# One layer of a streaming encoder: tokens turned by halves, sums of weights moved one block forward, state updates on quarters of rows

## The chip, the core and the metric

The kernel runs on one core of one Trainium2 chip, in one launch. The metric is device time in microseconds (us), the median of several executions. One further execution is recorded by the hardware profiler, and all lines of a profile come from that one.

The engines have short names in the profile: PE is the matrix engine (TensorE), PEld its loads of stationary operands, DVE the vector engine, ACT the scalar engine, POOL GpSimd, and SP the engine that here issues most of the DMA transfers.

## What is computed

The reference is one layer of a hybrid encoder. It gets a prompt of 2048 tokens and a batch of 8 samples with 16 tokens each, all 1024 wide:

```
for (x, states) in (prompt, empty), (samples, carried):
    q, k, v, o, i, f, qa, ka, va = split(x @ w_in)
    hm = sigmoid(o) * head_norm(mlstm(q, k, v, i, f, C0, n0, m0))   # 4 heads x 128
    ha = window_attention(rope(qa), rope(ka), va, caches, sinks)    # 8 q heads, 2 kv heads x 64
    h  = layer_norm(alpha * x + concat(hm, ha) @ w_out)
    u  = h @ w_up                                                   # 1024 -> 2 * 2816
    c  = b_conv + causal_conv3(u)
    a, g = split(c)
    y  = layer_norm(alpha * h + (silu(g) * a) @ w_down)
```

The outputs are y for prompt and samples, and the new states: the memory C, n, m of the mLSTM, the last keys and values, and the last two rows of u. For each sample and head, the state of C with n beside it is updated as `decay * C + sum over tokens of weight * k v`; this is the part that the change calls the batch's states.

## The kernel before, in words

The 128 tokens of the samples form a tile of their own (tile 16) beside 16 prompt tiles of 128 tokens. Four stages follow one another on PE.

1. **Input projection**, four blocks of four prompt tiles each (`IBLOCKS`), the first with the sample tile as well. It is done in the manner of Strassen: each output group g (0 to 4) of a block is seven products s with sums of weight quarters and of token quarters (`i_product`, L703), and each 32-bit product is made of three products with operands split into a high and a low part. PE is at this from the start to about 628 us.
2. **Output projection**, five blocks (L222 to L224), to about 910 us.
3. **Up projection** (`f_ups`, L1853), three token blocks of 5 or 6 tiles, 22 column groups j, seven products each, to about 1849 us. It also applies the conv and the gate.
4. **Down projection** (`f_downs`, L2065), to about 2315 us.

Into the first two stages the recurrences are woven: window attention, the chunks of the mLSTM and the sample's step (`t_sample`) are generators, and a planner (`Chains`) puts their next part behind a product, by a cost and a due time that each `yield` names. The order on PE is the order of the code. On the other engines a scheduler places the instructions, by priority and by when their inputs are ready; DMA transfers are issued from SP's queue, unless ACT is named, and wait there in order.

These places matter for the change:

- **The batch's states** (`t_sample`, L1426 to L1448). For each of the 4 heads, `weighted` makes v times each sample's weight for all 128 tokens (L1426, 8 samples x 129 columns, in three pieces of 3, 3 and 2 samples). PE computes the read-out `pnum` (L1440, L1443), POOL scales the old state (L1444), PE makes three products of all 128 rows (L1447), and DVE adds these to the state (L1448). Weights are zero except for a sample's own 16 tokens, so in a product over 128 rows only 16 rows of each sample's columns count.
- **Sums of weights** (`d_sums`, L843 to L855). The down projection, also in the manner of Strassen, needs sums of quarters of w_down. For each of 11 row pairs, step 0 loads two tiles of 512 KB into buffers shared with the block's tokens (`xr1`, `xr3`), step 1 subtracts four times on DVE, step 2 stores the two results to DRAM. Before, the first eight are spread over blocks 2 and 3 of the input projection: in each of the groups 0 to 3 the three steps stand behind products 6, 5, 3 (6, 2, 5 in group 3). The last three follow in the output projection.
- **Passage to the up projection** (`run`, L263 to L276; `f_hT`, L1690; `f_tokens`, L1719). While the last output block runs, `f_hT(0)` loads six tiles of normalised tokens on ACT's queue, PE turns each of them in two halves of 512 columns (L1713), and ACT copies the result into `hraw` (L1714). `f_tokens` then forms the token operands: a step 1, 7, 6, 2, 5, 3 or 4 splits a quarter into high and low (L217 on ACT, L218 on DVE), a step t1 to t4 subtracts quarters in place (L1728 to L1734). All steps that the first products need are called at one point, i == 15. `f_next` forms the weight operands, with sums at L1772 to L1775 from the tiles `wv` and `wg`, loaded at L1752 and L1754.
- **Passage to the down projection** (end of `f_ups`). `d_weights` loads a piece of w_down and splits it, and `d_tokens` forms the token operands from the quarters `r1` to `r4` (L2017 to L2027). Both are called behind the last seven products of the up projection.
- **Loads of the down projection** (`d_begin`, `d_load`). A table says behind which call of `d_tokens` each piece of a quarter is loaded. For the first block the second quarter is loaded in one go where `f_downs` begins.

Of the kernel before, what the change touches and what calls it, by code (L numbers as in the profile page):

```python
# [8 lines left out]
F32 = mybir.dt.float32  # L9
# [5 lines left out]
P = 128  # L15
D = 1024
KD = D // P
SEQ = 2048
DB = 8
DS = 16  # L20
# [5 lines left out]
NFF = FF // P  # L26
# [178 lines left out]
class Prog:  # L205
# [20 lines left out]
    def run(self):  # L226
        PS = bass.MemoryType.PSUM
        nb = len(OBLOCKS)
        with ExitStack() as es:
            def enter(*a, **k):  # L230
                cm = self.pool(*a, **k)
                return cm.__enter__(), cm
            close = lambda cm: cm.__exit__(None, None, None)
            self.cp = es.enter_context(self.pool("const"))
            self.dp = es.enter_context(self.pool("dram", space=bass.MemoryType.DRAM))
            es.enter_context(self.tc.manual_schedule(engines={mybir.EngineType.PE}))
            self.setup()
# [12 lines left out]
            wx, wxcm = enter("wx1sb")  # L250
            self.unit_more(wx)
            self.mp, mcm = enter("osb")
            self.o_setup()
            for b in range(nb - 1):
                chains.weave(self.late_done(self.o_block(b)))
            chains.until(NPT - 1)
            chains.drain()
            close(tpcm)
            close(tcm)
            self.fp, fcm = enter("fsb", side="right")  # L260
            self.fup, fpcm = enter("fup", 3, PS)
            self.f_setup()
            dense = self.o_block(nb - 1)  # L263
            first = self.f_hT(0)
            next(first)
            n = 0
            for i, _ in enumerate(dense):
                if i >= 2:
                    next(first, None)
                if i == 15:  # L270
                    self.f_tokens(0, 1, "t1", "t3", 7, "t2", 6)

                if i >= 22 and n < (2, 4, 5)[min((i - 22) // 4, 2)]:
                    self.f_next()
                    n += 1
            for _ in first:  # L276
                pass
            assert not self.norms
            close(mcm)
            close(wxcm)  # L280
            close(xcm)

            self.wx, wxcm = enter("wx2sb")
            self.f2, f2cm = enter("f2sb")
            self.f3, f3cm = enter("f3sb")
            self.f_ups(n)
            close(f3cm)
            close(f2cm)
            self.f2, f2cm = enter("dsb")
            self.f_downs()  # L290
            for cm in (f2cm, wxcm, fpcm, fcm):
                close(cm)
# [293 lines left out]
    def i_dense(self):  # L586
# [34 lines left out]
        for item in self.items:  # L621
# [56 lines left out]
            with self.tc.issue_after(behind) if behind and b == 0 else nullcontext():  # L678
                self.advance()

            if b >= nb // 2 and g < last:

                steps = (6, 2, 5) if g == last - 1 else (6, 5, 3)
                if s in steps:
                    self.d_sums(sums, steps.index(s))
                    sums += s == steps[2]
        self.sums = sums
        self.logs_of(nb - 1)
        self.chains.hold = False
# [672 lines left out]
    def t_sample(self):  # L1362
# [52 lines left out]
            nc.gpsimd.memset(q, 0.0)  # L1415
        yield 1900, 6000
        num = []
        last = lambda w, h, b0, n: w[:, h, DS - 1::DS].rearrange("p (b o) -> p b o", o=1)[:, b0:b0 + n].to_broadcast([P, n, 129])

        def weighted(h):  # L1420

            vws = []
            for tag, b0 in zip((("qh", "ql", "qa"), ("mixa", "v1", "hn"))[h % 2], (0, 3, 6)):
                nb = min(3, DB - b0)
                vw = self.work(tag, [P, nb, 129], bufs=2 if tag == "v1" else 1, name="vws")
                V.tensor_mul(vw, v1[:, h:h + 1, :].to_broadcast([P, nb, 129]), last(dt, h, b0, nb))  # L1426
                vws.append((vw, b0, nb))
            return vws
        vws = weighted(0)
        for j in range(2):  # L1430
            ps = self.bank([P, 2, 129], "pnum")
            for i in range(2):
                h = 2 * j + i
                cn = states[h]
                if h + 2 < MH:
                    states.append(state(h + 2))
                q = qm[h % 2]
                dg = bass.AP(q.tensor, q.offset, [list(q.ap[0]), [64, DB // 2], [32 + DS, 2], [1, DS]])
                V.tensor_copy(dg, qw[:, h].rearrange("p (c b l) -> p c b l", b=2, l=DS))
                nc.tensor.matmul(ps[:, i], sd[:, h], v1[:, h], start=True, stop=False, skip_group_check=True)  # L1440
                for r in range(2):
                    for c in range(DB // 2):
                        nc.tensor.matmul(ps[32 * c:32 * c + 32, i], q[:, 2 * c + r], cn[:, 2 * c + r], start=False, stop=r == 1, skip_group_check=True)  # L1443
                nc.gpsimd.tensor_mul(cn, cn, last(wi, h, 0, DB))  # L1444
                for vw, b0, nb in vws:
                    pc = self.bank([P, 3, 129], "pcs")
                    nc.tensor.matmul(pc[:, :nb].rearrange("p b e -> p (b e)"), ktok[:, h], vw.rearrange("p b e -> p (b e)"), start=True, stop=True)  # L1447
                    V.tensor_add(cn[:, b0:b0 + nb], cn[:, b0:b0 + nb], pc[:, :nb])  # L1448
                nc.sync.dma_start(a["cn_s"][:, h], cn)
                vws = weighted(h + 1) if h + 1 < MH else None  # L1450
                yield 2800, 3500
            num.append(ps)
        hn = self.m_norm(num, emt, og)
        load = self.swa_dma(t)
# [235 lines left out]
    def f_hT(self, b):  # L1690

        nc, fp = self.nc, self.fp
        self.hraw[b] = R = fp.tile([P, KD, 768], F32, name="hraw", tag="hraw", bufs=1)
        tiles = FBLOCKS[b]
        hs = {}


        tags = ["hst", "hst"] if b else ["hh1", "hl1", "hh7", "hl7", "hh6", "hl6"]

        def load(ti):  # L1700
            if ti < len(tiles):
                tag = tags[ti] if ti < len(tags) else "hst"
                hs[ti] = fp.tile([P, D], F32, name="hst", tag=tag, bufs=2 if tag == "hst" else 1)
                (nc.sync if b else nc.scalar).dma_start(hs[ti], self.zh[tiles[ti]])

        for ti in range(len(tags)):
            load(ti)
        yield
        for ti in range(len(tiles)):
            for i in range(2):  # L1710
                ps = self.fup.tile([P, 4, P], F32, name="fht", tag="fht", bufs=2)
                for k in range(4):
                    nc.tensor.transpose(ps[:, k], hs[ti][:, (4 * i + k) * P:(4 * i + k + 1) * P], self.ident)  # L1713
                nc.scalar.copy(R[:, 4 * i:4 * i + 4, ti * P:(ti + 1) * P], ps)  # L1714
                if i == 1:
                    load(ti + len(tags))
                yield

    def f_tokens(self, b, *steps):  # L1719
# [74 lines left out]
    def f_ups(self, n):  # L1794
# [11 lines left out]
        for i, (b, j, s) in enumerate(self.seq):  # L1806
# [23 lines left out]
                self.f_tokens(b + 1, *{1: (1, "t1", "t3"), 7: (7, "t2"), 6: (6,), 2: (2,), 5: (5, "t4"), 3: (3,), 4: (4,)}[s])  # L1830
            if b == nb - 1 and j == NFF - 3 and s == 6:
                self.d_begin()
            if b == nb - 1 and j == NFF - 1 and s not in (1, 7):
                self.d_weights()
                if s != 4:
                    self.d_tokens()
        nc.sync.dma_start(self.a["conv_p"], self.prev.rearrange("p v j r -> p (v j) r"))
        nc.sync.dma_start(self.a["conv_s"], self.convs.rearrange("p v j b r -> p (v j) b r"))

# [110 lines left out]
    def d_begin(self):  # L1950
        nb = len(FBLOCKS)
        self.dseq = [(b, s, u) for b in range(nb) for s in (DLAST if b == nb - 1 else DORDER) for u in range(len(DUNITS))]
        self.dw, self.df, self.dr, self.in_down = {}, {}, {}, False
        self.nw = self.nt = self.ring = 0

        self.dq = {}
        nu = len(DUNITS)
        for u in range(nu):
            self.d_load(0, 1, u)
            for b in range(nb):  # L1960
                n = 7 * nu * b + u
                for q, at in ((1, n - 2 * nu + 4), (2, n - nu + 4), (3, n + 4), (4, n + 4)):
                    if b or q > 2:
                        self.dq.setdefault(at, []).append((b, q, u))

    def d_shape(self, b):
# [65 lines left out]
    def f_downs(self):  # L2032
# [6 lines left out]
            nc.sync.dma_start(t, a[n].to_broadcast([P, D]))  # L2039
            ln2.append(t)  # L2040
        self.in_down = True
        for u in range(len(DUNITS)):
            self.d_load(0, 2, u)
        for n in sorted(n for n in self.dq if n <= self.nt):
            for l in self.dq.pop(n):
                self.d_load(*l)
# [121 lines left out]
```

## Time and profile before

| | us |
|---|---|
| median of 3 executions | 2321.95 |
| lowest, highest | 2318.91, 2327.77 |
| profiled execution | 2324.55 |
| its span, first to last instruction | 2322.7 |
| DVE, ACT, POOL busy | 1818.9, 1274.3, 261.3 |

The span is 1.85 us shorter than the profiled execution's own time. The mean granted clock of PE is 0.996 of the full one. The DMA engines moved 272 GB/s on average.

How to read the lines: a group names the source line, engine, operation, the tile written and the tiles read. A row of a timeline begins with the start and the length in us; a bracket at its end gives the time for which its engine stood idle before it and what released it. A row of stretches has the length, then the busy time of PE, PEld, DVE, ACT and POOL with the number of instructions, then the granted clock of PE (1.00 is the full one), the mean busy share of the 16 DMA engines, and GB/s. Matmuls overlap in the pipeline, so the time from one start to the next tells more than a length does.

### The profile page before, as it was taken

The page shows a single profiled execution, that of the slowest core. Times are in us where ns is not written, and L with a number is a line of the kernel's source. Part 1 is how long each engine was busy: PE and PEld are TensorE (multiplying, and loading weights), DVE is VectorE, ACT ScalarE, POOL GpSimd, SP SyncE. Part 2 cuts the span into 40 slices and gives each one's busy share as a digit, 9 for nine tenths or more (in the row PEclk, how much of TensorE's full clock was granted, in tenths as well). Part 3 has the DMA queues.
Part 4 walks back from the last instruction along what each step waited for, and adds up shares of the span by engine and source line. Part 5 has one row for each costly group of instructions (what it writes and reads, how often), then busy time and mean ns, then how long its engine had stood idle before and what let it go on. Part 6 is the DMA issues. An engine that isn't in the chain of part 4 may idle for free. (4 is left out here: it accounts for less than half of the span.)

```text
span 2322.7 us, 39853 instructions
## 1 busy us (share of the span) xinstructions
PE 2287.1 (98%) x14293; PEld 2095.7 (90%) x14293; DVE 1818.9 (78%) x3189; ACT 1274.3 (55%) x2409; POOL 261.3 (11%) x477
## 2 busy tenths in 40 slices
PE   8999999999999999999999999999999999999998
PEld 8999989989877778999999999999999978888876
DVE  8777587787788888998778767678766786895987
ACT  5453466776766655555556545555555544444442
POOL 0001000000011111121102101013111200100200
PEclk9999999999999999999999999999999999999999
DMA  7888999999977757788777888978888776756743
GB/s 278 295 303 292 304 316 334 309 304 346 323 260 229 247 193 259 291 326 306 282 292 270 307 301 312 315 265 285 303 293 265 228 282 203 257 178 217 254 157 108
DMA packets 299877, 632.38 MB, mean 272 GB/s; under 512 B 47836, under 2 KB 141088, under 8 KB 299680
## 3 DMA queue, kind: packets, MB, share of 16 engines
q1 hardware_dynamic: 295296, 616.14, 77.3%
q0 software_dynamic: 3520, 10.56, 1.4%
q10 hardware_dynamic: 864, 3.15, 0.3%
q8 instruction: 113, 1.85, 0.3%
q14 instruction: 84, 0.69, 0.1%
HBM read 458.11 MB, written 171.64 MB: 271 GB/s over the span
## 5 line engine op out<-in xcount | busy, mean ns | idle before, releaser
L1853 PE MATMUL fup<-hh,uw 128*128 128x384 f32 (+1 forms) x1848 | 479.8, 329 | 1.7 <-ACT ua L1874 0.9
L1853 PE MATMUL dps<-hh,uw 128*128 128x384 f32 (+1 forms) x1848 | 478.2, 328 | 2.9 <-DVE u L1884 2.0
L1853 PEld LDWEIGHTS fup<-hh,uw 128*128 128x128 f32 x1848 | 330.9, 188 | 3.2 <-ACT ua L1874 1.4
L1853 PEld LDWEIGHTS dps<-hh,uw 128*128 128x128 f32 x1848 | 329.9, 188 | 3.6 <-DVE u L1884 2.2
L1910 DVE SCALAR_TENSOR_TENSOR cc<-u,cw,cc 128x768 f32<-128x768 f32 (+1 forms) x264 | 258.0, 978 | 65.6 <-ACT cc L1908 56.0
L1853 PE MATMUL fup<-hl,uw 128*128 128x384 f32 (+1 forms) x924 | 303.2, 328 | 3.1 <-DVE hl L218 3.1
L1853 PE MATMUL dps<-hl,uw 128*128 128x384 f32 (+1 forms) x924 | 302.3, 327 | 0.0
L703 PE MATMUL dps<-w,oh 128*128 128x256 f32 x1344 | 254.6, 284 | 0.9 <-DMA w<-zws 0.9
L217 ACT CAST uw<-wraw 128x1024 fp32r<-128x1024 f32 x126 | 123.0, 979 | 224.8 <-PE dps L2065 120.1
L218 DVE TENSOR_TENSOR w<-wraw,w 128x1024 fp32r<-128x1024 f32 (+2 forms) x167 | 189.2, 1139 | 53.9 <-ACT w L217 52.4
L703 PEld LDWEIGHTS dps<-w,oh 128*128 128x128 f32 x1344 | 210.6, 188 | 12.2 <-issue 8.1
L217 ACT CAST w<-wraw 128x1024 fp32r<-128x1024 f32 (+2 forms) x167 | 163.2, 984 | 105.4 <-PE dps L703 40.0
L218 DVE TENSOR_TENSOR uw<-wraw,uw 128x1024 fp32r<-128x1024 f32 x126 | 142.2, 1130 | 64.4 <-ACT uw L217 64.2
L703 PE MATMUL dps<-w,ol 128*128 128x256 f32 x672 | 187.8, 279 | 0.0
L1853 PEld LDWEIGHTS fup<-hl,uw 128*128 128x128 f32 x924 | 174.0, 188 | 3.8 <-DVE hl L218 3.7
L703 PE MATMUL dps<-oh,w 128*128 128x256 f32 x896 | 170.3, 284 | 6.3 <-ACT mr L1151 3.6
L2065 PE MATMUL fup<-uw,fu 128*128 128x512 f32 x726 | 174.0, 396 | 1.6 <-DVE uw L218 1.6
L1853 PEld LDWEIGHTS dps<-hl,uw 128*128 128x128 f32 x924 | 173.5, 188 | 0.0
L2065 PEld LDWEIGHTS fup<-uw,fu 128*128 128x128 f32 x726 | 136.3, 188 | 34.9 <-DVE uw L218 2.1
L2065 PE MATMUL dps<-uw,fu 128*128 128x512 f32 x660 | 165.3, 396 | 1.1 <-DVE uw L218 1.1
L1908 ACT ACTIVATE cc<-u,cw 128x768 f32<-128x768 f32 (+1 forms) x132 | 132.2, 1001 | 56.9 <-DVE u L1890 25.7
L703 PEld LDWEIGHTS dps<-oh,w 128*128 128x128 f32 x896 | 141.4, 190 | 13.0 <-issue 4.1
(322 smaller groups left out, 4575.6 us busy)
## 6 DMA issues: line engine op xcount, KB each, us to landing
uw<-zw SPq DMA_DIRECT2D x176, 512.0 KB, 5.2
zw<-uw SPq DMA_DIRECT2D x88, 512.0 KB, 3.4
w<-zws SPq DMA_DIRECT2D x72, 512.0 KB, 6.3
wv<-wup SPq DMA_DIRECT2D x66, 512.0 KB, 4.8
wraw<-wi SPq DMA_DIRECT2D x65, 512.0 KB, 5.0
wraw<-zt SPq DMA_DIRECT2D x60, 512.0 KB, 4.1
wraw<-wdn SPq DMA_DIRECT2D x45, 512.0 KB, 4.2
wraw<-wo SPq DMA_DIRECT2D x40, 512.0 KB, 4.7
```

Of the source, the lines that this page charges most:

```text
L217: nc.scalar.copy(hi, src)
L218: nc.vector.tensor_sub(lo, src, hi.bitcast(F32))
L703: mm(o, l, r, start=s in (1, 7) and c == k == i == 0, stop=k == 3 and i == 2, skip_group_check=True)
L1853: mm(ps, l[:, k], r[:, k], start=s in (1, 7) and k == 0 and i == 0, stop=k == 3 and i == 2, skip_group_check=True)
L1908: S.activation(c[:, v], u[:, 2:2 + n], AF.Identity, bias=w[3], scale=w[2])
L1910: V.scalar_tensor_tensor(c[:, v], u[:, i:i + n], w[i], c[:, v], op0=ALU.mult, op1=ALU.add)
L2065: mm(ps, l[:, k, c], r[:, k], start=s in (1, 4, 7) and u == 0 and k == 0 and i == 0, stop=u == nu - 1 and k == n - 1 and i == 2, skip_grou ...
```

## The change

The arithmetic result is the same; work is cut and placed in another way.

1. `t_sample`: the weighted v is made and multiplied on quarters of rows. Quarter c holds the tokens of samples 2c and 2c + 1, so each product has 32 rows and the 258 columns of those two samples. Four products, each with its own PSUM tile, take the place of three, and DVE adds two samples at a time. The cost that the chain names to the planner goes from 2800 to 2000.
2. `d_sums`: its steps stand in groups 0 to 2 of blocks 1 to 3, behind products 7, 3 and 4, until eight are made.
3. `f_hT` and `f_tokens`: the six tiles of block 0 lie in four other buffers, with eight loads instead of six. The left halves of all tiles are turned first, then the right halves of tiles 3 to 5, then of 0 to 2. The steps of `f_tokens` are called at three points (i of 4, 7 and 10).
4. `f_ups`: `d_weights` and `d_tokens` are called by the number of products left.
5. `d_begin`: the second quarter's loads are in the table, and the third and fourth come three calls later.

```diff
@@ run
-                if i == 15:
-                    self.f_tokens(0, 1, "t1", "t3", 7, "t2", 6)
+                if i in (4, 7, 10):
+                    self.f_tokens(0, *{4: (1,), 7: ("t1",), 10: ("t3", 7, "t2", 6)}[i])
@@ i_dense
-            if b >= nb // 2 and g < last:
-                steps = (6, 2, 5) if g == last - 1 else (6, 5, 3)
-                if s in steps:
-                    self.d_sums(sums, steps.index(s))
-                    sums += s == steps[2]
+            if b and g < last - 1 and sums < NK2 - 3 and s in (7, 3, 4):
+                self.d_sums(sums, (7, 3, 4).index(s))
+                sums += s == 4
@@ t_sample
         def weighted(h):
-            vws = []
-            for tag, b0 in zip((("qh", "ql", "qa"), ("mixa", "v1", "hn"))[h % 2], (0, 3, 6)):
-                nb = min(3, DB - b0)
-                vw = self.work(tag, [P, nb, 129], bufs=2 if tag == "v1" else 1, name="vws")
-                V.tensor_mul(vw, v1[:, h:h + 1, :].to_broadcast([P, nb, 129]), last(dt, h, b0, nb))
-                vws.append((vw, b0, nb))
-            return vws
+            vw = self.work(("qh", "ql")[h % 2], [P, 2, 129], name="vws")
+            for c in range(DB // 2):
+                r = slice(32 * c, 32 * c + 32)
+                V.tensor_mul(vw[r], v1[r, h:h + 1, :].to_broadcast([32, 2, 129]), last(dt[r], h, 2 * c, 2, 32))
+            return vw
...
-                for vw, b0, nb in vws:
-                    pc = self.bank([P, 3, 129], "pcs")
-                    nc.tensor.matmul(pc[:, :nb].rearrange("p b e -> p (b e)"), ktok[:, h], vw.rearrange("p b e -> p (b e)"), start=True, stop=True)
-                    V.tensor_add(cn[:, b0:b0 + nb], cn[:, b0:b0 + nb], pc[:, :nb])
+                for c0 in (0, 2):
+                    pc = [self.bank([P, 2, 129], "pcs") for _ in range(2)]
+                    for c in range(2):
+                        r = slice(32 * (c0 + c), 32 * (c0 + c) + 32)
+                        nc.tensor.matmul(pc[c].rearrange("p b e -> p (b e)"), ktok[r, h], vws[r].rearrange("p b e -> p (b e)"), start=True, stop=True)
+                    for c in range(2):
+                        b0 = 2 * (c0 + c)
+                        V.tensor_add(cn[:, b0:b0 + 2], cn[:, b0:b0 + 2], pc[c])
...
-                yield 2800, 3500
+                yield 2000, 3500
@@ f_hT, for b == 0
+            n = len(tiles) // 2
+            for ts, tags in ((range(n), ("hh6", "hl6")), (range(n, 2 * n), ("hh7", "hl7"))):
+                w = [fp.tile([P, 3, 512], F32, name="hst", tag=tag, bufs=1) for tag in tags]
+                for c, t in enumerate(ts):
+                    z = self.zh[tiles[t]].rearrange("p (i m) -> p i m", i=2)
+                    at = [((2 * c + i) // 3, (2 * c + i) % 3) for i in range(2)]
...
+            for t, i in [(t, 0) for t in range(2 * n)] + [(t, 1) for t in (*range(n, 2 * n), *range(n))]:
+                transposed(t, i, hs[t, i])
+                yield
@@ f_ups
-            if b == nb - 1 and j == NFF - 1 and s not in (1, 7):
+            left = len(self.seq) - i
+            if left in (8, 7, 5, 3, 1):
                 self.d_weights()
-                if s != 4:
-                    self.d_tokens()
+            if left in (9, 8, 7, 6):
+                self.d_tokens()
@@ d_begin
-                for q, at in ((1, n - 2 * nu + 4), (2, n - nu + 4), (3, n + 4), (4, n + 4)):
-                    if b or q > 2:
+                for q, at in ((1, n - 2 * nu + 4), (2, n - nu + 4 if b else u + 2), (3, n + 7), (4, n + 7)):
+                    if b or q > 1:
                         self.dq.setdefault(at, []).append((b, q, u))
@@ f_downs
-        for u in range(len(DUNITS)):
-            self.d_load(0, 2, u)
```

More of the change, by code (lines that the diff above doesn't have):

```diff
@@ L1417, in t_sample @@
         num = []
-        last = lambda w, h, b0, n: w[:, h, DS - 1::DS].rearrange("p (b o) -> p b o", o=1)[:, b0:b0 + n].to_broadcast([P, n, 129])
+        last = lambda w, h, b0, n, p=P: w[:, h, DS - 1::DS].rearrange("p (b o) -> p b o", o=1)[:, b0:b0 + n].to_broadcast([p, n, 129])
         def weighted(h):
-            vws = []
-            for tag, b0 in zip((("qh", "ql", "qa"), ("mixa", "v1", "hn"))[h % 2], (0, 3, 6)):
-                nb = min(3, DB - b0)
-                vw = self.work(tag, [P, nb, 129], bufs=2 if tag == "v1" else 1, name="vws")
-                V.tensor_mul(vw, v1[:, h:h + 1, :].to_broadcast([P, nb, 129]), last(dt, h, b0, nb))
-                vws.append((vw, b0, nb))
-            return vws
+            vw = self.work(("qh", "ql")[h % 2], [P, 2, 129], name="vws")
[3 more added lines that the diff above has]
+            return vw
         vws = weighted(0)
@@ L1695, in f_hT, with transposed @@
         hs = {}
-        tags = ["hst", "hst"] if b else ["hh1", "hl1", "hh7", "hl7", "hh6", "hl6"]
+        def transposed(ti, i, src):
+            ps = self.fup.tile([P, 4, P], F32, name="fht", tag="fht", bufs=2)
+            for k in range(4):
+                nc.tensor.transpose(ps[:, k], src[:, k * P:(k + 1) * P], self.ident)
+            nc.scalar.copy(R[:, 4 * i:4 * i + 4, ti * P:(ti + 1) * P], ps)
+        if b == 0:
+            n = len(tiles) // 2
[4 more added lines that the diff above has]
+                    at = [((2 * c + i) // 3, (2 * c + i) % 3) for i in range(2)]
+                    for i, (a, k) in enumerate(at):
+                        hs[t, i] = w[a][:, k]
+                    if c == 1:
+                        for i, (a, k) in enumerate(at):
+                            nc.scalar.dma_start(hs[t, i], z[:, i])
+                    else:
+                        nc.scalar.dma_start(w[at[0][0]][:, at[0][1]:at[0][1] + 2], z)
+            yield
+            for t, i in [(t, 0) for t in range(2 * n)] + [(t, 1) for t in (*range(n, 2 * n), *range(n))]:
+                transposed(t, i, hs[t, i])
+                yield
+            return
         def load(ti):
             if ti < len(tiles):
[L1702 to L1706, printed above, removed]
+                hs[ti] = fp.tile([P, D], F32, name="hst", tag="hst", bufs=2)
+                nc.sync.dma_start(hs[ti], self.zh[tiles[ti]])
+        for ti in range(2):
             load(ti)
@@ L1710, in f_hT @@
             for i in range(2):
[L1711 to L1714, printed above, removed]
+                transposed(ti, i, hs[ti][:, i * 512:(i + 1) * 512])
                 if i == 1:
-                    load(ti + len(tags))
+                    load(ti + 2)
                 yield
```

## The prediction, made before the changed kernel had run

> **What bounds the kernel now.** I read the page's first part, then what TensorE waits for, then the clock around those waits. The page gives share and busy time of each engine:
>
> ```profile
> PE 2287.1 (98%) x14293; PEld 2095.7 (90%) x14293; DVE 1818.9 (78%) x3189; ACT 1274.3 (55%) x2409; POOL 261.3 (11%) x477
> ```
>
> TensorE is busy for 2287.1 of 2322.7 us, so this kernel is its own matmul stream plus 35.6 us. A change can gain by shortening the stream, or by taking waits out of those 35.6 us. The second view names the waits (total, times, longest):
>
> ```profile
> PE dps L703 <- ACT mr L1151: 3.6, 1, 3.6
> PE fup L1853 <- DVE hl L218: 3.1, 2, 2.5
> PE dps L1853 <- DVE u L1884: 2.0, 1, 2.0
> PE fup L2065 <- DVE uw L218: 1.6, 1, 1.6
> ```
>
> A wait can cost more than itself. The table of stretches (length, busy time of PE, PEld, DVE, ACT, POOL, granted clock, DMA share, GB/s) shows 3.4 us at half clock behind the first two:
>
> ```profile
> 329.60:333.00 3.40, 3.21 (x15) 3.21 (x16) 3.40 (x10) 1.74 (x6) 0.00 (x0) 0.50 1.16 331
> 920.10:923.50 3.40, 3.40 (x12) 3.40 (x12) 3.40 (x4) 0.00 (x0) 0.00 (x0) 0.50 0.39 160
> ```
>
> Half of 3.4 us is 1.7 us lost, so the first wait is worth 3.6 + 1.7 = 5.3 us and the second 2.5 + 1.7 = 4.2. The third has no such stretch. The Trainium skill ("TensorE: Matmul & The Clock Gate", Part 1) puts the fall to half clock after an idle window of about 3.4 us. The second row disagrees, as it follows an idle time of 2.5 us; by the page, removing that wait would be worth 2.5 instead of 4.2.
>
> **1. Batch states on quarters of rows (L1426 to L1448).** Per head, three full-height products of 387, 387 and 258 columns become four of 32 rows and 258 columns. In time order (start, length), one head before, and 64-row score products beside it:
>
> ```profile
> 198.31 0.65 PE L1443 MATMUL pnum<-cns,qm 128*32 128x129 f32 x16
> 198.89 2.00 PE L1447 MATMUL pcs<-vws,kw 128*128 128x387 f32 x6
> 200.54 0.47 PE L703 MATMUL dps<-oh,w 128*128 128x256 f32 x1
> ...
> 342.56 0.28 PE L703 MATMUL dps<-ol,w 128*128 128x256 f32 x1
> 342.68 0.28 PE L703 MATMUL dps<-oh,w 128*128 128x256 f32 x1
> 342.89 0.39 PE L1302 MATMUL psc<-kringh,qh 64*128 64x256 f32 x2
> 343.12 0.28 PE L1302 MATMUL psc<-kringl,qh 64*128 64x256 f32 x2
> 343.24 0.28 PE L1302 MATMUL psc<-kringh,ql 64*128 64x256 f32 x2
> ```
>
> Six passes (each product runs as two) take 200.54 - 198.89 = 1.65 us for 2 x (387 + 387 + 258) = 2064 columns, 0.80 ns a column; one pass of 258 is 0.206. The score rows say that different rows work side by side: x2 with 64 rows each start every 0.12 us, the 0.12 that one full-height product of 256 columns takes between 342.56 and 342.68. Bounds: nothing side by side, 8 x 0.206 = 1.65, gain 0; all four quarters side by side, 2 x 0.206 = 0.41, gain 1.24 a head, 5.0 in all. I take the middle: both passes of a quarter use the same rows, so only a quarter's second pass runs beside the next one's first, in 5 steps, 1.03 us, gain 0.62 a head. From this goes the change of shape: 342.68 to 342.89 is 0.21 where 0.12 is usual, so 0.09 to enter another shape; the section now has one more change at each head, 0.1 each. (0.62 - 0.1) x 4 = **-2.1**. A rule of the Trainium skill speaks against this edit ("TensorEngine Tiling (Array Packing)", Key Properties): changing the tiling mode drains TensorE. The 0.09 agrees; with a drain at both ends of each section the sum would be -1.8.
>
> VectorE's part, whole groups:
>
> ```profile
> L1426 DVE TENSOR_TENSOR vws<-v,dt x12: 411/547/1602, 191.6 to 210.0; 128x387 f32<-128x387 f32 x8, 128x258 f32<-128x258 f32 x4
> L1448 DVE TENSOR_TENSOR cns<-cns,pcs x12: 408/543/558, 201.4 to 222.8; 128x387 f32<-128x387 f32 x8, 128x258 f32<-128x258 f32 x4
> ```
>
> Twelve become sixteen of 258 columns at 0.41: 6.6 us for each line, where 8 x 0.55 + 4 x 0.41 = 6.0 stood. That is 1.2 us more on an engine which is idle for 14.9 of these 50 us (35.12 busy, row below): cost 0. Were that cover gone, it costs its 1.2.
>
> **2. Sums of weights from the second block on (d_sums).** Each of the 11 sums loads two tiles of 512 KB, subtracts four times on VectorE, and stores two. Eight lay in blocks 2 and 3; now three are in each of blocks 1 and 2 and two in block 3. A sum's first subtraction stands in VectorE's queue, so a late tile holds all behind it:
>
> ```profile
> L849 DVE TENSOR_TENSOR txy<-txy x11: 636/684/693, 310.5 to 833.4; 128x512 f32<-128x512 f32 x11
> DMA to landing us min/median/max: 3.2/5.1/8.6
> ...
> 324.69 0.69 DVE L849 TENSOR_TENSOR txy<-txy 128x512 f32<-128x512 f32 x1 [3.45 <-DMA txy<-wdn]
> 328.12 0.17 ACT L1151 ACTIVATE mr<-pnum 128x2 f32<-128x2 f32 x1 [2.69 <-DVE bst L1148]
> 329.79 0.58 PE L703 MATMUL dps<-oh,w 128*128 128x256 f32 x1 [3.56 <-ACT mr L1151]
> ...
> 513.08 0.69 DVE L849 TENSOR_TENSOR txy<-txy 128x512 f32<-128x512 f32 x1 [1.08 <-DMA txy<-wdn]
> 578.20 0.50 PE L703 MATMUL dps<-w,oh 128*128 128x256 f32 x2 [0.52 <-DMA w<-zws]
> ```
>
> This is the kernel's dearest wait: the tile comes 3.45 us late, the statistics L1148 behind it start late, ScalarE's L1151 with them, and TensorE stands for 3.56. Does it go? The order of instructions in the changed kernel says no: a sum of block 2 still has its load behind the same store on SP and its subtraction at the same place of VectorE's queue, ahead of the same L1148. Only one load ahead of it has moved away. I give it 0.2 of its 5.3.
>
> Blocks 2 and 3 lose two sums, 4 MB of traffic in all. The two small waits nearest to these sums, at 517 (behind the 513.08 row; TensorE's gap there is about the 1.08 of that row) and 577 (0.52), I expect to shrink by 0.8 and 0.5. With the 0.2: **-1.5**, between 0 and -5.3 - 1.1 - 0.5 = -6.9.
>
> Block 1 gets three sums, 4 x 0.68 = 2.7 us of VectorE and 2 MB each. The room there:
>
> ```profile
> 165.00:200.00 35.00, 35.00 (x308) 34.01 (x307) 30.11 (x69) 17.93 (x28) 2.23 (x2) 1.00 0.84 287
> 200.00:250.00 50.00, 49.60 (x441) 46.30 (x440) 35.12 (x72) 15.91 (x35) 7.96 (x6) 1.00 0.88 315
> ```
>
> 6 MB at some 315 GB/s is 19 us of a channel that is 12 to 16% free over 85 us (about 12 us): it fills up, as it does now behind 329.60 (share 1.16). VectorE has 4.9 and 14.9 us free for 2.7 + 5.4, so it fits, tightly in the first stretch. Setting the new loads into the order by hand, with 5.1 us to landing, the first and second subtraction come about 1 us before their data, and VectorE's delay reaches TensorE only where what follows is needed soon. Bounds: 0, if each finds its tile, and 3 x 5.3 = 16 if each repeats the 324.69 row. The row it is nearest to is 513.08: a subtraction 1.08 late, TensorE late by about that. One or two such: **+1.5**.
>
> **3. Tokens turned by halves, loads spread (f_hT, f_tokens).** At the passage to the up projection VectorE must build the first tokens, and its queue is late (start, length, idle before in brackets):
>
> ```profile
> 887.39 0.59 ACT L1714 COPY hraw<-fht 128x512 f32<-128x512 f32 x1 [0.55 <-PE fht L1713]
> 890.27 1.47 ACT L217 CAST hh<-hraw 128x1536 fp32r<-128x1536 f32 x1
> 890.35 0.69 DVE L1615 SCALAR_TENSOR_TENSOR ymix<-ymix,dps 128x512 f32<-128x512 f32 x1 [0.88 <-PE dps L224]
> 894.77 1.23 DVE L218 TENSOR_TENSOR w<-wraw,w 128x1024 fp32r<-128x1024 f32 x1 [1.23 <-ACT w L217]
> 896.02 0.33 SPq L1754 DMA_DIRECT2D wg<-wup  x1
> 897.02 1.23 DVE L218 TENSOR_TENSOR w<-wraw,w 128x1024 fp32r<-128x1024 f32 x1 [1.03 <-ACT w L217]
> 898.17 1.75 DVE L1728 TENSOR_TENSOR hraw<-hraw 128x1536 f32<-128x1536 f32 x1
> 918.03 1.75 DVE L218 TENSOR_TENSOR hl<-hraw,hh 128x1536 fp32r<-128x1536 f32 x1
> 919.84 0.49 PE L1853 MATMUL fup<-hl,uw 128*128 128x384 f32 x1 [2.50 <-DVE hl L218]
> ```
>
> Before, the cast at 890.27 needs five turned halves and the subtraction at 898.17 eleven; now three and six. Turns come about 1.13 us apart (a copy of 0.59 and an idle 0.55), so the cast comes 2.3 us earlier, and the subtraction can fill the idle 0.88 + 1.23 + 1.03 = 3.1 us ahead of 898.17. Work in VectorE's queue up to 918.03 stays the same, so the last token split ends up to 3.1 us sooner. Not all of it lasts: the new order has the weight sums of L1773 ahead of the last token split, and they wait for the weight that SP issues at 896.02. With a landing between the 3.2 and 5.1 us of the row in part 2 they can't start before about 900; with that I count 1.6 of 3.1. TensorE's wait falls from 2.5 to 0.9, and at 0.9 I expect no half-clock stretch: -1.6 - 1.7 = **-3.3**. Bounds: 0, and -4.2, all that is there. The loads are eight instead of six on ScalarE's queue, on an engine that is idle for 45% of the span: 0; without that cover, two issues more at the 0.33 us of the 896.02 row, 0.7.
>
> **4. Last product of the up projection (d_weights, d_tokens).** In the changed order VectorE, ScalarE and SP have the same sequence there as before: 0, the 2.0 us wait for L1884 stays.
>
> **5. Down projection loads.** The second quarter's loads go between others, and one VectorE operation leaves from ahead of the weight split that TensorE awaits:
>
> ```profile
> 1888.76 0.96 DVE L2025 TENSOR_TENSOR r<-r,r 128x768 f32<-128x768 f32 x1
> 1889.63 1.82 DVE L218 TENSOR_TENSOR uw<-wraw,uw 128x1024 fp32r<-128x1024 f32 x2
> ```
>
> The split starts 1889.63 - 1888.76 = 0.87 sooner: **-0.9**, between 0 and -1.6 (the whole wait).
>
> **Sum.** -2.1 - 1.5 + 1.5 - 3.3 + 0 - 0.9 = -6.3. The profiled execution took 2324.55 us (span 2322.7 and 1.85 around it): 2318.25. It lay 2.6 above the median of 2321.95, so the forecast is **2315.7 us**. About 0.5%, 11.6 us, is what a measurement of this kernel can tell from no change.
>
> **Rivals.**
> - **The dearest wait goes after all.** If the load that moved away lets the tile land 3.5 us sooner, 324.69 finds its data: 5.1 more, 2310.6. For it: sums come less densely, and the tile missed by 3.45 us where landings spread from 3.2 to 8.6. Against: the same places in both queues, and the full DMA engines there.
> - **Block 1 becomes what block 2 was.** Each new sum repeats the 324.69 row. It decides where a tile lands over 3 us after its subtraction's turn, with a product's eviction or the sample's chain right behind it on VectorE: 16 instead of 1.5, **2330.2, slower than before**. For it: 0.84 to 0.88 of the DMA engines are taken already, 30.11 of 35 us of VectorE in the first stretch. Against: from 200 on VectorE idles for a third of the time, which takes up a wait of 1 to 2 us.
> - **The passage only changes its wait.** If the weight issued at 896.02 lands 1.5 us later than I count, VectorE stands at L1773 and no gain is left: 2319.0.
> - **Quarters one after the other.** If passes on different quarters don't overlap at this size, the edit gives nothing: 2.1 back, 2317.8.
>
> **Chances.** Forecast 0.42; dearest wait gone 0.2; block 1 slow 0.15; passage 0.13; quarters serial 0.1. The unknown costs' ends add up to 5.0 + 6.9 + 4.2 + 1.6 = 17.7 below the profiled time and 16 above it; with two or three of them together the range that holds 8 in 10 is 2304 to 2329, the dearest-wait rival with a good part 1 at its lower end, block 1's slow case for two of three sums at its upper. Faster by over 0.5% (below 2310.3) needs the first rival and a little more, or nearly all lower ends: half of the 0.2, and 0.13 out of the other cases, 0.23. Slower by over 0.5% (above 2333.6): three quarters of block 1's slow case, with one more half-clock stretch or none of the gains: 0.12. Within: 0.65.
>
> **What would show it.** Right: pcs sections of about 1.1 us; no 0.50 stretch near 920 and a wait on hl under 1.2; the 3.5 us wait on L1151 near 326 still there; L849 idle in block 1 under 2 us each time; the wait on L1884 unchanged. Wrong: new TensorE waits over 2 us or half clock between 165 and 300, a uw or L1773 idle over 2 us near 900, pcs sections of 1.65.

## The result, and the profile after

The changed kernel is slower. Its median is 2340.19 us (six executions, 2332.49 to 2345.3), against 2321.57 us before (six executions). The ratio is 1.0069 with a 95% interval of 1.0053 to 1.0085. The forecast was 2315.7 with a range of 2304 to 2329, so the time lies outside the range and on the other side of before.

The profiled execution took 2333.96 us, with a span of 2332.1. It is one of the two quick ones of its kind and shows 9.4 us of the loss; the four slower executions have a lower mean granted clock (0.988 to 0.991, against 0.993 here), which is what more of the half-clock stretches shown below would give.

First the page of the changed kernel (busy us of each engine), then what TensorE waits for (total, times, longest):

```profile
PE 2287.2 (98%) x14301; PEld 2098.0 (90%) x14301; DVE 1821.5 (78%) x3197; ACT 1272.8 (55%) x2409; POOL 263.6 (11%) x477
```

```profile
PE dps L702 <- DMA w<-zws: 5.9, 8, 1.3
PE dps L702 <- DVE wraw L547: 4.2, 1, 4.2
PE pcs L1447 <- DVE hn L1153: 3.1, 1, 3.1
...
PE dps L1878 <- DVE u L1909: 2.0, 1, 2.0
...
PE pnum L1437 <- DVE cns L1450: 1.7, 1, 1.7
PE fup L1878 <- DVE hl L218: 1.7, 2, 1.1
...
PE dps L702 <- ACT mr L1150: 1.0, 1, 1.0
...
PE fup L2088 <- DVE uw L218: 0.6, 1, 0.6
```

The dearest wait of before (on L1151, now L1150) is down from 3.6 to 1.0, hl from 2.5 to 1.1, uw of the down projection from 1.6 to 0.6. The three rows at the top are new or have grown: weights that come late (w<-zws), a token operand (wraw at L547), and the states' products (pcs, with pnum behind it). Before, late weights had cost little:

```profile
PE dps L703 <- DMA w<-zws: 0.9, 2, 0.5
```

The stretches of block 1 in the changed kernel, and four stretches at about half clock:

```profile
200.00:225.00 25.00, 20.21 (x160) 17.95 (x160) 19.56 (x35) 4.41 (x7) 5.04 (x3) 0.80 0.86 301
225.00:250.00 25.00, 23.62 (x230) 22.42 (x229) 16.99 (x40) 8.38 (x17) 3.06 (x3) 1.00 0.92 327
250.00:275.00 25.00, 21.45 (x152) 19.40 (x152) 9.60 (x19) 7.62 (x18) 1.15 (x1) 0.80 0.77 235
275.00:300.00 25.00, 19.83 (x170) 19.00 (x169) 8.67 (x17) 8.12 (x18) 1.40 (x1) 0.93 0.77 270
...
213.40:223.60 10.20, 7.13 (x34) 6.20 (x29) 5.82 (x9) 2.10 (x3) 1.70 (x1) 0.51 0.99 344
264.60:274.80 10.20, 10.20 (x66) 9.04 (x65) 1.89 (x3) 2.54 (x4) 0.00 (x0) 0.51 0.57 206
291.90:295.30 3.40, 2.86 (x13) 2.86 (x14) 0.00 (x0) 0.00 (x0) 0.00 (x0) 0.53 1.04 396
319.30:322.70 3.40, 3.17 (x14) 3.17 (x15) 3.40 (x5) 3.36 (x7) 0.00 (x0) 0.52 0.60 205
```

TensorE was busy for 23.4 us of these 27.2 us at about half clock, so they cost some 12 us; before, this part of the kernel had one stretch of 3.4 us. The waits cause the rest.

To place the loss, I compared the start of each TensorE instruction with the start of the same one before (the order is the same but for pcs). Between two points, the growth of that difference is what the stretch lost:

| stretch, by the starts of before | us lost |
|---|---|
| 165 to 302 (block 1) | 26.7 |
| 302 to 345 (where the wait on L1151 was) | -2.8 |
| 345 to 906 | -5.3 |
| 906 to 932 (passage to the up projection) | -3.0 |
| 932 to 1880 | -3.7 |
| 1880 to 1910 (down projection's split) | -1.0 |

So everything after block 1 goes as forecast or better, and block 1 loses 26.7 where +1.5 stood in the sum for it and -2.1 for the states, which lie in it too. (Of the 5.3, 1.6 is a half-clock stretch near 688 that this execution lacks, and most of the 3.7 is small gaps of before between 1630 and 1710; neither belongs to an edit. Another 1.3 of the 5.3 lie between 880 and 900, where the halves are turned: all five runs with the new turning win 1.1 to 1.3 there, those with the old one at most 0.7. At 165 it was 1.2 ahead, so the rows add up to 9.7 at 1910.)

What happens there: the states' first and third head, in time order, then VectorE's row that releases the third, with what stands ahead of it on VectorE and what GpSimd (POOL) does beside it.

```profile
198.97 0.72 PE L1447 MATMUL pcs<-vws,kw 32*128 32x258 f32 x8
199.61 0.39 PE L702 MATMUL dps<-oh,w 128*128 128x256 f32 x1
...
212.00 0.49 PE L1437 MATMUL pnum<-v,sd 128*128 128x129 f32 x2 [1.73 <-DVE cns L1450]
213.00 0.71 PE L1447 MATMUL pcs<-vws,kw 32*128 32x258 f32 x6
216.78 1.19 PE L1447 MATMUL pcs<-vws,kw 32*128 32x258 f32 x2 [3.07 <-DVE hn L1153]
...
212.86 3.39 DVE L1424 TENSOR_TENSOR vws<-v,dt 32x258 f32<-32x258 f32 x4
213.18 1.92 POOL L1441 TENSOR_TENSOR cns<-cns,wi 128x1032 f32<-128x1032 f32 x1 [6.33 <-PE pnum L1440]
216.28 0.35 DVE L1153 SCALAR_TENSOR_TENSOR hn<-pnum,bmv,og 128x128 f32<-128x128 f32 x1
```

The first head's section is 0.64 us long (198.97 to 199.61) where it was 1.65: quarters do work side by side. But the third head's fourth quarter waits 3.07 us for VectorE's last read of the first pnum tile. Four pcs tiles and two pnum tiles are six, and the pool of PSUM buffers that holds both (`tps`; PSUM is where TensorE puts its results) has five; before, three and two were just five. The length of the wait comes from VectorE's order: ahead of that last read it makes the next head's four weighted products, of 0.42 us each, and the one that starts at 213.29 takes 2.09 us, beside GpSimd's scaling of the state. No run puts that read first.

And the tokens of the next block, with the rows of SP, VectorE and TensorE that belong together:

```profile
257.14 0.43 SPq L853 DMA_DIRECT2D zt<-txy  x1
281.20 0.99 SPq L537 DMA_DIRECT2D xr<-xq  x2
...
289.94 1.22 DVE L547 TENSOR_TENSOR wraw<-xr 128x1024 f32<-128x1024 f32 x1
291.26 0.36 PE L702 MATMUL dps<-w,oh 128*128 128x256 f32 x1 [4.22 <-DVE wraw L547]
```

Two of the token loads of block 2 are issued at 281.20, when TensorE is already about to need them. Before, they left early:

```profile
163.29 1.37 SPq L536 DMA_DIRECT2D xr<-xq  x1
...
173.75 0.42 SPq L536 DMA_DIRECT2D xr<-xq  x1
...
273.42 1.23 DVE L546 TENSOR_TENSOR wraw<-xr 128x1024 f32<-128x1024 f32 x1
```

The four loads of before went out between 163.29 and 173.75 and had 100 us in hand. The sums borrow two of these four buffers and take their place in SP's queue.

### The profile page after: what moved, and what is told of

The parts are those of the page before. It is cut to its first block, busy times and chain, and to the rows that moved or that the text cites. A ratio compares the mean times of both kernels' runs of the same rounds, so it can differ in the third digit from the quotient of the medians.

```text
span 2332.1 us, 39871 instructions
## 1 busy us (share of the span) xinstructions
PE 2287.2 (98%) x14301; PEld 2098.0 (90%) x14301; DVE 1821.5 (78%) x3197; ACT 1272.8 (55%) x2409; POOL 263.6 (11%) x477
## 5 line engine op out<-in xcount | busy, mean ns | idle before, releaser
L702 PE MATMUL dps<-w,oh 128*128 128x256 f32 x1344 | 260.3, 288 | 10.1 <-DMA w<-zws 5.9
L702 PEld LDWEIGHTS dps<-w,oh 128*128 128x128 f32 x1344 | 214.4, 191 | 23.4 <-issue 9.6
L702 PEld LDWEIGHTS dps<-oh,w 128*128 128x128 f32 x896 | 142.3, 191 | 11.1 <-issue 5.0
```

The lines of the kernel that those rows point to most:

```text
L702: mm(o, l, r, start=s in (1, 7) and c == k == i == 0, stop=k == 3 and i == 2, skip_group_check=True)
```

## The experiments

Each run is given as its median less that of before on the same chip (2322.2 to 2323.9), and, from its profile, what it lost between 165 and 302 in the way of the table above. The runs of one kernel spread over 4 to 13 us, so a profile's loss is that of one execution.

### Which edit

**Sums back in their old place**, all else as changed:

```diff
-            if b and g < last - 1 and sums < NK2 - 3 and s in (7, 3, 4):
...
+            if b >= nb // 2 and g < last:
...
+                steps = (6, 2, 5) if g == last - 1 else (6, 5, 3)
...
```

> The changed kernel with only the sums of weights put back to blocks 2 and 3. Theory A (sums): the three sums in block 1 hold VectorE, behind it the stores on SP and behind these the weight loads; then the 16 us that TensorE loses between 230 and 300 are gone, the wait on L1151 near 326 is back, and the median is near 2317. Theory B (banks): two pnum tiles and four pcs tiles need six PSUM banks of the five, and all that follows comes out of that wait; then TensorE's waits on pnum and pcs near 212 and 213 (1.7 and 3.1) and the half clock behind them stay, and the median stays above 2330.

Measured: 2316.89, that is 7.1 faster than before (ratio 0.9976, 0.9967 to 0.9985); 4.4 lost in block 1. Without the moved sums the kernel isn't slower. Theory B's wait, though, needs no moved sums:

```profile
PE pcs L1450 <- DVE hn L1156: 3.1, 1, 3.1
```

The 3.1 us at pcs are there with the sums put back, in the same size.

**States back**, sums moved: the loop over `c0` gives way to the old loop over `vws`.

> The changed kernel with only the batch's states put back to three products of all rows. Theory A: the waits at 212 and 213 with their half clock go (about 5 less), the waits for weights between 240 and 300 stay, median 2333 to 2337. Theory B: what was lost between 230 and 300 was the wake of the bank wait, so both go and the median is near 2320.

Measured: 2332.98, 9.0 slower than before (1.0049, 1.0033 to 1.0065); 20.5 lost in block 1. Theory A's 2333 is met: 20.5 of the 26.7 in block 1 stand without the bank wait (the wait for a free PSUM buffer), though by the median only 9.0 of the 18.6.

**Both back:**

> The changed kernel with sums and states both put back: the passage by halves and the down loads alone. Both theories: faster than before by the 4.2 of the passage and the 0.9 of the down projection, 2316 to 2317. If it isn't faster than before, these gains of the profile were chance.

Measured: 2317.11, 6.8 faster (0.9974, 0.9964 to 0.9984); 0.3 lost in block 1. The gains at the two passages are real: its profile wins 3.1 between 906 and 932 and 1.0 between 1880 and 1910, as the changed kernel does.

**Sums alone**, put into the kernel before:

> The kernel before with only the sums moved one block forward. Theory A: 16 lost in block 1, 4 to 5 won at 326, so 2331 to 2335. Theory B: no bank wait, so nothing is lost in block 1 and the 326 wait is gone: 2317 to 2322.

Measured: 2335.95, 12.0 slower (1.0065, 1.0052 to 1.0078); 25.2 lost in block 1, in an execution that is the slowest of its runs, 7.3 above the median. Two of its waits:

```profile
PE dps L700 <- DMA w<-zws: 10.4, 9, 4.1
PE pgr L1002 <- DVE g L993: 2.6, 1, 2.6
```

Theory A comes near the time, theory B as the only cause is out. The second row, near 179, is VectorE behind its late subtractions; with 6.8 us at half clock around it, it makes 5.9 of the loss, up to 190. The first row belongs to what follows.

### What about the sums: work, bytes or places

**Subtractions on GpSimd** (`V.tensor_sub` to `nc.gpsimd.tensor_sub`):

> As the run with the sums alone moved (12 slower than before), but the four subtractions of each sum run on GpSimd. Theory H (hold): VectorE stands at a subtraction whose tile is late, and what is queued behind it, evictions, SP's stores and then the weight loads, comes late; then the loss in block 1 is gone and the time is at or under that of before, 2317 to 2324. Theory D (traffic): 6 MB more through DMA engines that are 84 to 88% busy make the weight loads land late by themselves; then it stays near 2336.

Measured: 2356.97, 34.7 slower; 20.8 lost in block 1. This was no clean test. All eleven sums went to GpSimd, where one subtraction (512 columns) took 1.3 us or more instead of 0.68 and stood in front of other work there:

```profile
L846 POOL TENSOR_TENSOR txy<-txy x11: 1286/1613/5177, 170.1 to 842.7; 128x512 f32<-128x512 f32 x11
...
  DMA txy<-wdn: 58.0, 11
```

GpSimd stood for 58 us at tiles not yet landed, with its part of the recurrences behind them. Still, with VectorE free of them, block 1 lost nearly as much.

**No subtraction in block 1:**

```diff
         if step == 1:
+            if k < 3:
+                return
```

> As the run with the sums alone moved, but the three sums of block 1 load and store without subtracting (the stored sums are left out, the traffic is whole). Theory H: the loss in block 1 is gone, 2317 to 2324. Theory D: it stays near 2336.

Measured: 2335.03, 12.7 slower (1.0058, 1.0041 to 1.0075), by the median as much as with the subtractions. Theory H, which was mine in the prediction, falls as the main cause. Its profile lost 12.2 in block 1, nothing of it up to 224: the wait near 179 is gone, and with it the 5.9 that it cost in the run above. These are two stretches of that run, and its waits:

```profile
165.00:200.00 35.00, 35.00 (x308) 33.88 (x307) 30.03 (x66) 16.87 (x27) 3.25 (x2) 1.00 0.98 350
200.00:225.00 25.00, 25.00 (x220) 22.25 (x219) 17.09 (x42) 6.39 (x11) 6.92 (x5) 1.00 0.98 353
```

```profile
PE dps L700 <- DVE wraw L546: 5.6, 1, 5.6
PE dps L700 <- DMA w<-zws: 3.6, 6, 0.9
```

With no subtraction on VectorE, the DMA engines are at a share of 0.98 for 60 us, and behind that, from 224 to 302, the time goes to late weights and late tokens.

**No traffic in block 1** (subtractions on cleared tiles; weights copied from DRAM to DRAM in place of the sums):

> As the run with the sums alone moved, but in block 1 the three sums only subtract, on tiles that GpSimd clears; their loads and stores are left out, and the weights themselves are copied in place of the sums in the last output block. VectorE's 2.7 us for each sum stay, and no tile is late. Theory H: no hold, only the work, so nearly all is gone, 2317 to 2325. Theory D: all gone, 2317 to 2322. If it stays near 2336, VectorE's work alone is too much for the place.

Measured: 2341.0, 18.7 slower. Here the experiment was badly built: the copies depended on nothing, and the scheduler put them into the first 20 us, where the profile lost 11.0 us before 165; and it put all subtractions between 175 and 194 of that execution, which cost 6.9. Behind that, up to 302 by the starts of before, it lost 0.7. So it only shows that the second part of block 1 loses next to nothing when it has neither the bytes nor subtractions.

**Thin sums**, built to mend that: transfers and subtractions stay, with 32 of 1024 columns.

```diff
-            nc.sync.dma_start(x, self.a["wdn"][k])
...
+            m = D
+            if k < 3:
+                m = 32
...
+            nc.sync.dma_start(x[:, :m], self.a["wdn"][k][:, :m])
...
```

> As the run with the sums alone moved (12 slower than before), but each of the three sums of block 1 loads and stores only 32 of 1024 columns (GpSimd clears the rest; the weights of the first two units are read in place of these sums). SP's number of transfers and VectorE's four subtractions stay, one part in 32 of the bytes stays. Theory D (bytes): nothing is lost from 190 to 302, and with the 326 wait relieved the time is 2318 to 2324. Theory X (place of the token loads and SP's queue): one token load still stands 86 places later in SP's order, so a wait of some 4 us and half clock stay, 2326 or more. Theory H (hold on VectorE): 2334 or more.

Measured: 2327.5, 5.3 slower than before (1.0019, 1.0006 to 1.0031), so 6.7 better than the sums alone; 5.9 lost in block 1 instead of 25.2, no token wait, and 2.7 on weights. The bytes are the larger part, with what hangs on them: the last token load leaves at 264 instead of 280. But 4.7 are still lost from 190 to 302, where theory D had nothing, and the time is over its 2324, so what remains (VectorE's work, more entries in SP's queue, GpSimd's clears) costs something too, and the wait on mr stays at 2.1:

```profile
PE dps L700 <- DMA w<-zws: 2.7, 4, 0.8
PE dps L700 <- ACT mr L1154: 2.1, 1, 2.1
```

**Token loads put early**, same bytes:

```diff
...
+                        if b != 1:
+                            self.x_load(b + 1, 1, 2, 3, 4)
...
+            if b == 1 and g == 1 and s == 4:
+                self.x_load(2, 1, 2, 3, 4)
...
```

> As the run without subtractions (12.7 slower than before), and in block 1 the third sum's four transfers go from DRAM to DRAM at the same places (so it borrows no token buffer; its values are left out), and the four token loads of block 2 are put in the code right behind the second sum's stores. Theory X (late tokens): sums that borrow xr1 and xr3 push the token loads of block 2 behind some 70 other transfers in SP's order, and the tokens come late; then the 5.8 us gap near 274 and its half clock go, about 9 less, 2324 to 2327. Theory D (traffic): the bytes are the same, so it stays at 2333 to 2336.

Measured: 2329.49, 6.9 slower (1.0032, 1.0015 to 1.0049), between the two theories. The profile says why: the wait of 5.6 for tokens is gone, and one of 4.0 for weights is there instead.

```profile
242.24 0.80 PE L703 MATMUL dps<-w,oh 128*128 128x256 f32 x2 [4.01 <-DMA w<-zws]
```

It lost 11.1 in block 1, with 12.2 in the run without subtractions: no change that one profile of each can show. The 5.9 between the two medians came from elsewhere or from the spread; I leave that open. With the tokens first, it is the weights that come late.

**Two sums instead of three, tokens early** (`and (b > 1 or g < 2)`):

> As the run with the sums alone moved (12 slower than before), with two whole sums in block 1 instead of three (three in block 3), and the token loads of block 2 right behind the second one. Theory X with the hold on VectorE for the rest: the wait near 286 goes with its half clock (8 less) and with the third sum its part of the late weights; what stays is the hold at 176 (2.8 and half clock): 2322 to 2328. Theory D: a third of the traffic gone, a third of the loss: 2331 to 2333.

Measured: 2329.87, 7.2 slower (1.0043, 1.0027 to 1.006); 8.6 lost in block 1. That lies between the two theories, a little nearer to theory D: two thirds of the bytes, and still a loss, with one wait of 3.3 us for weights and one of 1.9 near 178 behind VectorE.

### The states, and a better kernel

**States alone**, put into the kernel before:

> The kernel before with only the batch's states on quarters of rows. Theory B (banks) for this edit: each head's section is 1.0 us shorter, 4 in all, but the fourth pcs tile of the third head waits for a pnum bank, 3 us and a half-clock stretch: within 2 of before, 2320 to 2325, and a wait on pcs near 213. Without the bank theory: 4 faster, 2318.

Measured: 2324.53 (1.0009, 0.9998 to 1.0020): no difference that can be told. The wait is there as forecast:

```profile
211.44 0.71 PE L1448 MATMUL pcs<-vws,kw 32*128 32x258 f32 x6
215.22 1.19 PE L1448 MATMUL pcs<-vws,kw 32*128 32x258 f32 x2 [3.07 <-DVE hn L1154]
```

**Quarters for two heads**, the other two in three products as before, so that five tiles are enough:

```diff
         def weighted(h):
+            if h < 2:
...
```

> The kernel before with quarters of rows for heads 0 and 1 only. Theory B: at most five banks are asked for, no wait at pcs, 2 faster: 2319 to 2321. Without it: the same wait as with all four heads.

Measured: 2319.6 (0.9986, 0.9973 to 0.9999), 4.9 below the run with four heads, each by its own before; no wait at pcs. Theory B holds for this edit, with intervals of the two runs that just touch.

**Sums in blocks 2 and 3, with the new spacing, and two heads on quarters:**

> The changed kernel with the sums in groups 0 to 3 of blocks 2 and 3, but behind products 7, 3 and 4, and with quarters of rows for heads 0 and 1 only (heads 2 and 3 as before, so that pnum and pcs need at most five PSUM banks). If the wider spacing from load to subtraction is what spares the 326 wait, that wait is under 1 and the run is 5 below the 2317 of the run with the sums put back. If the wait went only since fewer sums lie there, it stays at 2317. Theory B: no wait at pcs near 213.

Measured: 2317.17, 5.1 faster than before (0.9979, 0.9967 to 0.9991), much the same as with the sums simply put back. The wait near 326 is still 2.6 there, so the wider spacing alone doesn't remove it:

```profile
PE dps L702 <- ACT mr L1150: 2.6, 1, 2.6
```

```profile
208.53 0.38 PE L1445 MATMUL pnum<-v,sd 128*128 128x129 f32 x2
208.84 0.65 PE L1448 MATMUL pnum<-cns,qm 128*32 128x129 f32 x16
209.42 2.00 PE L1463 MATMUL pcs<-vws,kw 128*128 128x387 f32 x6
```

Here the third head runs without a bracket, so without a wait. But the 4.9 between two heads and four don't show here: two heads, four (the sums put back, 2316.89) and none (both put back, 2317.11) lie together. That gain rests on the pair of runs in the kernel before. This kernel, the one with the sums put back and the one with both edits put back lie at 2316.9 to 2317.2, and all three are below both kernels.

## Why the prediction was wrong, step by step

- **Block 1's sums: the step that failed.** "One or two such: +1.5" was mis-sized. With the sums alone block 1 lost 25.2 in the profile, and the whole kernel 12.0 by its median. I had worked out the shortage (19 us of traffic, about 12 us of room) and then priced it by VectorE's stall at a late subtraction. Those stalls came in about the size that I took (1.44, 2.05, 1.99 and 0.53 us in block 1 of the changed kernel), with one TensorE wait of 1.56 behind them; the loss lies elsewhere. Leaving out the subtractions left the median where it was (+12.7), while leaving out the bytes took more than half of it away (+5.3). The bytes show as late weights and late tokens, neither of which I had priced.
- **The token loads** were missing from the sum. The buffers are shared, I had noted that in the change, and yet didn't follow the four loads in SP's order: they go from 163 to 173 before, to 191 and 281 after. The run with the loads put early shows that this alone isn't the cost, since weights come late in their place.
- **States: the gain was put too low, and a wait was missing.** The section went from 1.65 to 0.64 (1.01 at the second head), a gain of 1.0 a head where 0.52 net was taken, so more runs side by side than I took; 0.41 was the lower bound. But the sixth PSUM tile costs 3.1 us and a half-clock stretch, which eats the gain (+1.9 with four heads, -3.0 with two, each against before). I counted matmul columns and not tiles alive at once. VectorE's weighted products, put at 6.0 and 6.6 us by the usual length, were busy for 8.4 and 10.1: the longest of 1602 ns stood in the row shown, and I passed over it.
- **Drain between shapes.** The rule of the Trainium skill that was weighed, that a change of tiling mode drains TensorE ("TensorEngine Tiling (Array Packing)", Key Properties), changes little: with all that it spends on changes of shape the section is still 1.0 shorter.
- **The dearest wait** I expected to stay. It went in the changed kernel (3.6 to 1.0) and was 2.0 to 3.0 in most runs, 3.7 with both edits back. Its half-clock stretch comes and goes. Why it shrinks was not settled. The gains of 0.8 and 0.5 near 517 and 577 came out as 0.8 and 0.8, but the run with the sums back in their old place wins 0.6 and 0.8 there too: that term came right by luck.
- **Passage and down projection were right.** hl went from 2.5 to 1.1 (0.9 forecast), there is no half clock near 932, 3.0 gained in the profile (3.3 forecast); uw gave 1.0 (0.9 forecast); L1884's wait of 2.0 stayed. These edits alone give 6.8 by the median, where 4.2 were forecast; 4.1 of it lie at the two places, and 1.3 between 880 and 900, where the halves are turned, a place that the sum didn't have. The 1.7 for the half clock is no fixed price: of ten runs with the old passage, all with the wait of 2.5, eight have a half-clock stretch behind it and two have none. VectorE does stand for the weight, as expected:

```profile
917.55 0.69 DVE L1796 TENSOR_TENSOR uw<-wv,wg 128x512 f32<-128x512 f32 x1 [1.48 <-DMA wg<-wup]
935.73 0.45 PE L1878 MATMUL fup<-hl,uw 128*128 128x384 f32 x1 [1.09 <-DVE hl L218]
```

- **Rivals.** "Block 1 becomes what block 2 was" had the place and the sign, and at 2330.2 was too small. Its condition, tiles over 3 us late, didn't arise (2.05 at most), and its mechanism (VectorE's queue) isn't the main one, as the run without subtractions shows; that it came nearest was luck. Of "the dearest wait goes" the wait did shrink, from 3.6 to 1.0. The passage kept its gain, and quarters don't run one after the other.

What stays open: how the loss in block 1 beyond the bytes (5.9 of 25.2) divides between VectorE's work, SP's queue and GpSimd's clears; and why the states cost nothing alone but took the kernel with the sums moved from +9.0 to +18.6. The wait of 3.07 us is the same with the sums moved or not. With them moved a wait of 1.7 on pnum joins it, and 10.2 us of half clock follow, against 6.8 and 3.4 in the two runs with the sums in their old place; whether that is all was not followed further.

## What to carry to other kernels

When work with transfers is moved to an earlier place, add its bytes to that place's share of the DMA engines first: here, where they were at 0.84 to 0.88 already, 6 MB more came back as late weights and tokens, in front of an engine that is 98% busy. Look up who else uses the borrowed buffers, and where their loads then stand in the issuing queue. When a product is cut into more pieces, count the PSUM tiles that are alive at once against the pool before counting the time saved.

## What the runs showed of the hardware

Products of 32 rows on different quarters ran in large part side by side: eight passes of 258 columns in 0.64 us, where 0.80 ns a column gives 1.65 one after the other and 0.41 four at a time. Waits that are short one by one can have a long stretch at about half clock behind them: 10.2 us from 264.6 on, behind two waits for weights of 1.35 and 0.72 us. And a VectorE product of 258 columns took 2.09 us instead of 0.42 where it started during GpSimd's scaling of the state (1.92 us); before, two of 387 columns took 1.60 us instead of 0.55 in the same place.
